# A two-layer decoder trunk on one core: rotary table and masks loaded behind the first four weight tiles, squares of the first norm ordered behind casts

## The chip, the cores and the metric

One Trainium2 chip, one NeuronCore of it. The metric is the device time of one execution in microseconds; the number told for a kernel is the median of its runs.

## The reference, cut to what matters

Two decoder layers on 256 tokens of width 2048, all in float32. Layer 0 is a norm, one wide input projection that feeds an RG-LRU group and an HGRN2 group of 8 heads, an output projection and an MLP; layer 1 has dilated attention in place of the two groups. The change touches only the first steps:

```python
h = x
hn = rms_norm(h, norm_mix[0])      # x * rsqrt(mean(x*x) + eps) * gain
proj = hn @ w_in                   # 2048 x 6144
x_lru, y_lru, q_h, f_h, v_h, g_h = jnp.split(proj, ...)
...
q = silu(q_raw); f = lower_bound + (1 - lower_bound) * sigmoid(f_raw)   # per HGRN2 head
```

The kernel multiplies by w_in before it knows the norm's factor: the gain is put on x beforehand, and the factor of each token (`rt`, and its transpose `rs`) is applied to the results.

## The kernel before, in words

Weights stream through the core in tiles of 128 x 2048 float32 (1024 KB). Each is loaded by SyncE's queue into a buffer `raw`, split by ScalarE into a rounded part `hi` (L104) and by VectorE into the rest `lo = raw - hi` (L105), in two halves of 1024 columns, and then used by TensorE in float32r matmuls (L187): activation-hi times hi, activation-lo times hi, activation-hi times lo. `raw`, `hi` and `lo` have three buffers each, so a new tile's cast to `hi` waits until TensorE is done with the tile three places before.

I number the weight tiles u0, u1, u2 and so on in the order of their use. u0 to u3 are the four tiles of the value group v0 (two PSUM accumulators, tokens on the partitions); u4, u5 and u6 are the q, f and g projections of HGRN2 head 0; u7 is the first RG-LRU projection; u8 to u10 are head 1. Every projection from u4 on takes one PSUM bank named `p` of a pool with three banks (`pmm`): v0 has the first and the second, u4 the third, u5 and u6 the first and second again, u7 the third again. A bank is free again when it has been read: v0's by the copy `vg` (L361), the banks of u4, u5 and u6 by the multiplication `hz = p * rs` (L425), whose factor `rs` (buffer `nr`, copied from PSUM at L379) comes from the first norm.

The opening (`fetch_first`) loads x and u0 to u3 in turns and in pieces: u0 in four pieces of 512 columns, u1 in two of 1024, u2 and u3 whole, each with its share of x ahead of it (L165 and L166). For each of the 16 blocks of x ScalarE writes the scaled rounded part into `bufa` (L248) and VectorE the rest (L249). `FirstNorm.add` squares each block of x on ScalarE (L280, tile `t`) and VectorE sums the squares in `q` (L283, L285); after the sixteenth, four pairs of small matmuls (L293) turn the sums into one number for each token, VectorE works out the reciprocal root in a chain of small operations (L295, L330 to L335), two transposes (L317) spread it, and ScalarE copies the result (L379). The transposes need the identity in `tab_` (L264), which also holds the rotary frequencies; the masks `msk` (L266) are read by the HGRN2 heads.

The order of instructions on each engine is fixed when the kernel is built, by a scheduler that goes by its own estimate of durations, by priorities (`high_priority`, `stream`, `urgent`) and by the dependencies it is given. `after(ins, names)` adds a dependency that costs no wait at run time and only fixes the order of two instructions on one engine. On the chip every engine works through its own list in order. SyncE's DMAs use eight semaphores in turn, so an issue also waits for the DMA eight places before.

Of the kernel before, what the change touches and what calls it, by code (L numbers as in the profile page):

```python
# [15 lines left out]
AF = mybir.ActivationFunctionType  # L16
# [25 lines left out]
def trunk_kernel(ctx, tc, x, xtok, cols, tab, masks, pos, fin, w_in, w_gate, w_out, w_qkv, w_o, w1, w2, out):  # L42
    nc = tc.nc
# [13 lines left out]
    V, A, T = nc.vector, nc.scalar, nc.tensor  # L57
# [8 lines left out]
    made = {}  # L66
# [10 lines left out]
    for step in ORDER.split():  # L77
        src, first, n = where[step[0]]
# [14 lines left out]
    class Weights:  # L93
# [7 lines left out]
        def split(self, at, n):  # L101
            h, l = self.part(at, n)
            w = self.raw[:, at:at + n]
            A.copy(h, w)  # L104
            i = V.tensor_tensor(l, w, h.bitcast(F32), OP.subtract)  # L105
            self.ins = getattr(i, "ins", i)

# [19 lines left out]
    def combine(u, src, i, what, i0):  # L127
        def load(name, j, home=wraw):
            held[name] = home.tile([P, 2048], F32, name="raw" if home is wraw else name)
            nc.sync.dma_start(held[name], src[j])  # L130

        def add(to, x, y):
            return V.tensor_tensor(held[to], held[x], held[y], OP.add)

        if what == "a":
            load("t1", i0 + 4, both)
            load("a", i)
            held["s"] = both.tile([P, 2048], F32, name="s")
            add("s", "a", "t1")
        elif what in ("n", "d"):  # L140
            load(what, i)
        def make(step=2048):
            made[u] = Weights(held[{"t1": "s", "t2": "s", "t3": "t1", "t4": "s"}.get(what, what)], step)

        ahead = units[u + 1][2:3] if u + 1 < len(units) else ()
        if ahead == ("t2",):
            load("c", i0 + 5)
            nc.gpsimd.dma_start(held["t1"], src[i0 + 5], accum_op=OP.add)
            add("s", "s", "c")
        make(2048 if src is w1 or what != "t2" else 0)  # L150
        if src is not w1 and what == "t2":
            waiting.append(made[u])
        if what == "c":
            nc.gpsimd.dma_start(held["s"], src[i0 + 1], accum_op=OP.add)

    def fetch_first():
        for u in range(4):
            at[0] += 1
            r = wraw.tile([P, 2048], F32, name="raw")
            src, i = units[u]  # L160
            n = (4, 2, 1, 1)[u]
            for m in range(n):
                ks = slice(4 * u + m * 4 // n, 4 * u + (m + 1) * 4 // n)
                ws = slice(m * 2048 // n, (m + 1) * 2048 // n)
                nc.sync.dma_start(xin[:, ks], x[:, ks])  # L165
                nc.sync.dma_start(r[:, ws], src[i][:, ws])  # L166
                if m == 0 and n > 1:
                    made[u] = Weights(r, 0)
                for k in range(ks.start, ks.stop):
                    split_to(bufa[:, k], xin[:, k], col("nmix0", k))  # L170
                if n > 1:
                    made[u].split(m * 2048 // n, 2048 // n)
                else:
                    made[u] = Weights(r, 1024)

    def unit(src, i):
        u = at[1]
        assert units[u][0] is src and units[u][1] in (None, i), (u, i)
        at[1] += 1
        if u + 2 >= at[0]:  # L180
            fetch()
        return made.pop(u)
# [24 lines left out]
    def after(ins, names):  # L207
        ins = getattr(ins, "ins", ins)
        for n in names:
            tc.add_manual_dep(ins, n, NOSYNC, reason="order on one engine")  # L210
        return ins.name
# [30 lines left out]
    def split_to(dst, src, gain=None):  # L242
        if gain is None:
            h, l = dst[..., :S], dst[..., S:]
            A.copy(h, src)  # L245
            V.tensor_tensor(l, src, h.bitcast(F32), OP.subtract)
        else:
            A.activation(dst[:, :S], src, AF.Copy, scale=gain)  # L248
            V.scalar_tensor_tensor(dst[:, S:], src, gain, dst[:, :S].bitcast(F32),  # L249
                                   op0=OP.mult, op1=OP.subtract)  # L250
# [9 lines left out]
    with tc.high_priority():  # L260
        nc.scalar.dma_start(c_, cols)
        fetch_first()
    tab_ = cst.tile([P, NTAB], F32, name="tab_")
    nc.sync.dma_start(tab_, tab)  # L264
    msk = cst.tile([P, NLEV, P], I8, name="msk")
    nc.sync.dma_start(msk, masks)  # L266
    ident = tab_[:, TC_ID:TC_ID + P]
    lnc = tab_[:, TC_LNC:TC_LNC + 384]
    epsc = cst.tile([P, 1], F32, name="epsc")
# [3 lines left out]
    class FirstNorm:  # L273
# [3 lines left out]
        def add(self, blk):  # L277
            self.n += 1
            q = wk.tile([P, S], F32, name="t1", bufs=2)
            A.activation(q, blk, AF.Square)  # L280
            if self.n == 1:
                self.ss.append(wk.tile([P, S], F32, name="q", bufs=1))
                V.tensor_copy(self.ss[0], q)  # L283
            elif self.n < KB:
                V.tensor_tensor(self.ss[0], self.ss[0], q, OP.add)  # L285
            else:
                self.ss.append(q)
# [293 lines left out]
    for step in ORDER.split():  # L581
        i = int(step[1])
# [324 lines left out]
    def values(i0):  # L907
# [16 lines left out]
        def final(n, j, bank):  # L924
            if (n, j) == (0, 1):
                with urgent():
                    A.activation(v[:, j, n], bank, AF.Copy, scale=rt[:, j:j + 1])
            elif (n, j) == (1, 0):
                add(n, j, bank, v[:, j, n], OP.subtract)
            else:  # L930
                add(n, j, bank, v[:, j, n], OP.add, scale=not n)
# [29 lines left out]
    with urgent():  # L961
        for j in range(2):
            m = tmp.tile([P, 1], F32, name="fm", bufs=2)
            r = tmp.tile([P, 1], F32, name="fr", bufs=2)
# [5 lines left out]
            i = V.scalar_tensor_tensor(m, ss[:, LAST:LAST + 1], 1.0 / D, m, op0=OP.mult, op1=OP.add)  # L970
            sums2.append(getattr(i, "ins", i).name)
            i = A.activation(t, m, AF.Sqrt)
# [6 lines left out]
        for j in range(2):  # L979
            for n, e in ((0, A), (LAST, V), (1, A if j else V), (3, V if j else A)):  # L980
# [4 lines left out]
                elif e is A:  # L985
                    i = A.activation(x_, x_, AF.Copy, scale=rr[j])
                    if n == 3:
                        after(i, roots[1:])
                else:
                    i = V.tensor_scalar(x_, x_, rr[j], None, op0=OP.mult)  # L990
# [118 lines left out]
```

## Time and profile before

| | |
|---|---|
| median of 3 runs | 2158.49 us (2158.27 to 2158.55) |
| the profiled execution's own time | 2158.39 us |
| its span | 2156.4 us, so 1.99 us lie around the span |
| TensorE matmul busy | 2140.6 us, 99% |
| VectorE busy | 1788.3 us, 83% |
| ScalarE busy | 1270.0 us, 59% |
| DMA | 485.64 MB, mean 225 GB/s |

In the profile PE is TensorE's matmuls, PEld its weight loads, DVE VectorE, ACT ScalarE, SP SyncE; a q behind an engine's name is its sequencer, which issues DMAs. All times count from the span's start. In a row of the timeline the first two numbers are the start and the duration in us, an x with a number tells how many instructions the row holds, and brackets give the idle time ahead of it and what ended that.

### The profile page before, as it was taken

The page shows a single profiled execution, that of the slowest core. Times are in us where ns is not written, and L with a number is a line of the kernel's source. Part 1 is how long each engine was busy: PE and PEld are TensorE (multiplying, and loading weights), DVE is VectorE, ACT ScalarE, POOL GpSimd, SP SyncE. Part 2 cuts the span into 40 slices and gives each one's busy share as a digit, 9 for nine tenths or more (in the row PEclk, how much of TensorE's full clock was granted, in tenths as well). Part 3 has the DMA queues.
Part 4 walks back from the last instruction along what each step waited for, and adds up shares of the span by engine and source line. Part 5 has one row for each costly group of instructions (what it writes and reads, how often), then busy time and mean ns, then how long its engine had stood idle before and what let it go on. Part 6 is the DMA issues. An engine that isn't in the chain of part 4 may idle for free.

```text
span 2156.4 us, 27736 instructions
## 1 busy us (share of the span) xinstructions
PE 2140.6 (99%) x11020; PEld 1831.1 (85%) x11020; DVE 1788.3 (83%) x2098; ACT 1270.0 (59%) x1415; POOL 61.9 (3%) x77
## 2 busy tenths in 40 slices
PE   9999999999999999999999999999999999999998
PEld 8999998888888888888888888888888888888886
DVE  7776787788888888889998897867988988888887
ACT  7444485566566566557665546456655755755764
POOL 0000000000000000000000000000000000000000
PEclk9999999999999999999999999999999999999999
DMA  8444445578878788887775546457778778788884
GB/s 320 157 157 158 156 157 214 177 234 273 247 241 258 255 247 239 277 246 236 247 258 196 175 160 232 157 183 227 236 241 278 243 241 264 254 247 244 265 262 153
DMA packets 68736, 485.64 MB, mean 225 GB/s; under 512 B 7664, under 2 KB 8432, under 8 KB 10624
## 3 DMA queue, kind: packets, MB, share of 16 engines
q1 hardware_dynamic: 58176, 410.89, 51.8%
q0 software_dynamic: 10144, 72.39, 18.1%
q8 instruction: 86, 1.41, 0.3%
q10 hardware_dynamic: 288, 0.61, 0.1%
q14 instruction: 42, 0.34, 0.0%
HBM read 481.76 MB, written 2.10 MB: 224 GB/s over the span
## 4 chain that ended last, share of the span: by engine, by line
PE 96%; DVE 2%; DMA 1%; ACT 1%; issue 0%; SPq 0%; DVEq 0%
PE p L187 66%; PE pd L187 12%; PE po L187 12%; PE pl L190 2%; PE pl L483 1%; DVE lo L105 1%; PE pt L187 1%; DMA raw<-in_w_in 1%; DMA raw<-in_w 0%; ACT hi L104 0%; PE pl L877 0%; PE po L898 0%; PE pd L890 0%; PE pd L467 0%; PE pl L876 0%
## 5 line engine op out<-in xcount | busy, mean ns | idle before, releaser
L104 ACT CAST hi<-raw 128x2048 fp32r<-128x2048 f32 (+2 forms) x468 | 683.8, 1484 | 552.1 <-PE p L187 345.4
L105 DVE TENSOR_TENSOR lo<-raw,hi 128x2048 fp32r<-128x2048 f32 (+2 forms) x468 | 816.7, 1760 | 221.9 <-ACT hi L104 206.3
L187 PE MATMUL p<-hi,bufb 128*128 128x512 f32 x1408 | 448.9, 391 | 0.5 <-ACT bufb L245 0.5
L187 PE MATMUL p<-hi,bufa 128*128 128x512 f32 x1136 | 366.4, 391 | 1.0 <-ACT hi L104 1.0
L187 PE MATMUL p<-bufa,hi 128*128 128x256 f32 (+1 forms) x1792 | 365.3, 317 | 0.1
L187 PEld LDWEIGHTS p<-hi,bufb 128*128 128x128 f32 x1408 | 264.3, 188 | 55.6 <-ACT bufb L245 0.7
L187 PEld LDWEIGHTS p<-bufa,hi 128*128 128x128 f32 x1792 | 294.2, 190 | 18.6 <-DVE hz L425 0.3
L187 PE MATMUL p<-lo,bufb 128*128 128x512 f32 x704 | 274.3, 390 | 0.7 <-DVE lo L105 0.7
L187 PE MATMUL p<-bufa,lo 128*128 128x256 f32 x1152 | 256.6, 287 | 0.0
L187 PEld LDWEIGHTS p<-hi,bufa 128*128 128x128 f32 x1136 | 213.5, 188 | 48.3 <-DVE y L727 2.4
L105 DVE TENSOR_TENSOR lo<-s,hi 128x2048 fp32r<-128x2048 f32 x102 | 233.1, 2286 | 17.9 <-ACT hi L104 15.8
L104 ACT CAST hi<-s 128x2048 fp32r<-128x2048 f32 x102 | 195.2, 1913 | 51.6 <-PE po L187 21.3
L187 PE MATMUL p<-lo,bufa 128*128 128x512 f32 x568 | 221.6, 390 | 1.8 <-DVE lo L105 1.8
L187 PEld LDWEIGHTS p<-bufa,lo 128*128 128x128 f32 x1152 | 189.7, 191 | 2.7
L187 PEld LDWEIGHTS p<-lo,bufb 128*128 128x128 f32 x704 | 132.2, 188 | 27.8 <-DVE lo L105 1.0
L187 PEld LDWEIGHTS p<-lo,bufa 128*128 128x128 f32 x568 | 106.8, 188 | 24.4 <-DVE lo L105 3.0
L187 PE MATMUL pd<-hi,bufa 128*128 128x512 f32 x288 | 95.3, 392 | 0.0
L187 PE MATMUL p<-hi,formx 128*128 128x512 f32 x288 | 94.9, 390 | 0.0
L105 DVE TENSOR_TENSOR lo<-t,hi 128x2048 fp32r<-128x2048 f32 x34 | 77.8, 2288 | 13.0 <-ACT hi L104 13.0
L187 PE MATMUL po<-hi,bufa 128*128 128x512 f32 x256 | 84.9, 393 | 0.0
L187 PE MATMUL p<-hi,formh 128*128 128x512 f32 x256 | 84.0, 389 | 0.0
L187 PE MATMUL pd<-hi,bufb 128*128 128x512 f32 x256 | 83.0, 389 | 0.0
(302 smaller groups left out, 2891.9 us busy)
## 6 DMA issues: line engine op xcount, KB each, us to landing
raw<-in_w SPq DMA_DIRECT2D x224, 1024.0 KB, 6.5
raw<-in_w_in SPq DMA_DIRECT2D x46, 1024.0 KB, 4.9
raw<-in_w_qkv SPq DMA_DIRECT2D x46, 1024.0 KB, 5.0
t<-in_w SPq DMA_DIRECT2D x32, 1024.0 KB, 6.4
t<-in_w POOLq DMA_DIRECT2D x32, 1024.0 KB, 8.8
s<-in_w POOLq DMA_DIRECT2D x32, 1024.0 KB, 9.2
raw<-in_w_out SPq DMA_DIRECT2D x16, 1024.0 KB, 4.9
raw<-in_w_o SPq DMA_DIRECT2D x16, 1024.0 KB, 4.9
```

The source lines that it names most:

```text
L104: A.copy(h, w)
L105: i = V.tensor_tensor(l, w, h.bitcast(F32), OP.subtract)
L187: chain[:] = [after(T.matmul(*args, **kw), chain)]
L190: chain[:] = [after(T.transpose(out_, in_, ident), chain)]
L483: T.matmul(pl[:, j], kq[:, js], halves(qp[:, js], c, True), start=True, stop=True)
```

## The change

Two things, both in the opening. First, the loads of `tab_` and `msk` get an order behind the last load of `fetch_first`, the weights of u3; before, they stood on SyncE's queue between the last piece of u0 and the first of u1. Second, each square of the first norm gets an order on ScalarE behind a cast of a weight tile: the squares 1 to 6 behind the last cast of u1, 7 to 12 behind that of u2, 13 to 16 behind that of u3. No operation is added or removed.

```diff
         def split(self, at, n):
             h, l = self.part(at, n)
             w = self.raw[:, at:at + n]
-            A.copy(h, w)
+            self.cast = after(A.copy(h, w), [])
...
+    loads, casts = [], []
+
     def fetch_first():
         for u in range(4):
...
                 nc.sync.dma_start(xin[:, ks], x[:, ks])
-                nc.sync.dma_start(r[:, ws], src[i][:, ws])
+                loads[:] = [after(nc.sync.dma_start(r[:, ws], src[i][:, ws]), [])]
...
                 else:
                     made[u] = Weights(r, 1024)
+            casts.append(made[u].cast)
...
-    nc.sync.dma_start(tab_, tab)
+    after(nc.sync.dma_start(tab_, tab), loads)
     msk = cst.tile([P, NLEV, P], I8, name="msk")
-    nc.sync.dma_start(msk, masks)
+    after(nc.sync.dma_start(msk, masks), loads)
...
             q = wk.tile([P, S], F32, name="t1", bufs=2)
-            A.activation(q, blk, AF.Square)
+            after(A.activation(q, blk, AF.Square), [casts[1 if self.n <= 6 else 2 if self.n <= 12 else 3]])
```

Because the scheduler lays out each engine's list anew with these orders, the lists of the built kernels differ beyond the lines that were touched, up to about the 290th row of TensorE's list; behind that they are the same. The prediction quotes from the new lists what it uses.

## The prediction

> **What bounds the kernel.** I read the page's busy shares and chain first.
>
> ```profile
> span 2156.4 us, 27736 instructions
> PE 2140.6 (99%) x11020; PEld 1831.1 (85%) x11020; DVE 1788.3 (83%) x2098; ACT 1270.0 (59%) x1415; POOL 61.9 (3%) x77
> PE 96%; DVE 2%; DMA 1%; ACT 1%; issue 0%; SPq 0%; DVEq 0%
> ```
>
> TensorE is busy for 99% of the span and carries 96% of the chain that ended last. So an edit in the opening counts by one thing: how much idle time of TensorE it takes away or adds. The second view is what TensorE waited for in the first 120 us, then the chain in order of time (start, length, what).
>
> ```profile
> PE p L187 <- DVE lo L105: 1.8, 3, 0.8
> PE po L259 <- DVE xp L535: 1.1, 1, 1.1
> PE p L187 <- ACT hi L104: 1.0, 2, 0.7
> ```
>
> ```profile
> 4.01 5.72 DMA raw<-in_w_in
> 9.73 0.02 issue
> 9.75 9.97 DMA raw<-in_w_in
> 19.72 0.02 issue
> 19.74 1.06 ACT hi L104
> 20.80 0.02 issue
> 20.82 1.24 DVE lo L105
> 22.06 0.04 issue
> 22.11 12.60 PE p L187 x61
> 34.70 0.79 PE pt L293 x8
> ...
> 42.54 0.22 PE pt L317 x2
> ...
> 52.47 0.45 PE pd L467 x4
> ```
>
> The chain is made of transfers until 19.72, when u2's weights have landed; then come u2's first cast, its remainder, and from 22.11 on TensorE without a break. Nothing that TensorE waits for lies between 22.11 and 120 us. So the opening has a gain to give only up to 22.11, and any new wait behind it is a loss in full.
>
> **Part one: table and masks behind u3.** The transfers are the limit there, by the windows (length, then busy time of PE, PEld, DVE, ACT, POOL, granted clock, DMA share, GB/s) and the table of DMA issues (the last number is the time from issue to landing).
>
> ```profile
> 6.20:10.00 3.80, 3.73 (x15) 2.55 (x14) 2.67 (x11) 2.57 (x6) 0.00 (x0) 1.00 1.00 324
> 10.00:15.00 5.00, 3.41 (x12) 2.10 (x12) 4.77 (x16) 4.27 (x11) 0.00 (x0) 1.00 1.01 351
> 15.00:20.00 5.00, 4.90 (x22) 4.06 (x23) 4.98 (x17) 3.77 (x9) 0.00 (x0) 1.00 1.02 423
> ```
>
> ```profile
> 4.49 0.43 SPq L264 DMA_DIRECT2D tab__181<-in_tab  x1
> 4.97 0.43 SPq L266 DMA_DIRECT2D msk<-in_masks  x1
> ...
> tab__181<-in_tab SPq DMA_DIRECT2D x1, 257.0 KB, 6.0
> msk<-in_masks SPq DMA_DIRECT2D x1, 80.0 KB, 5.7
> ```
>
> The DMA engines are full from 6.2 to 20, so what counts is the bytes ahead of u2's. u0's last piece landed at 9.73 (4.01 + 5.72); the table landed at 4.49 + 6.0 = 10.5 and the masks at 4.97 + 5.7 = 10.67. Together they held the transfers for 10.67 - 9.73 = 0.94 us. By bytes it would be 337 KB, 345 thousand bytes, at 423 to 324 GB/s: 0.82 to 1.06 us. Moved behind u3, they leave this time to u1, u2 and u3: u2 lands at about 18.8. Behind u2 come u3's x and weights, 1.57 MB, 3.7 us at 423 GB/s, so table and masks land at about 18.8 + 3.7 + 0.94 = 23.4. Their first readers are the two transposes (42.54 in the chain) and, for the masks, a head's work behind them: some 19 us of cover, cost nothing. If that cover were gone, the price would be the 0.94 us again.
>
> **Part two: squares behind the casts.** The squares leave ScalarE's and VectorE's lists ahead of u1.
>
> ```profile
> 12.14 0.71 ACT L280 ACTIVATE t<-xall 128x256 f32<-128x256 f32 x2
> 12.76 1.03 ACT L104 CAST hi<-raw 128x1024 fp32r<-128x1024 f32 x1
> 15.10 0.50 PE L187 MATMUL p<-lo,bufa 128*128 128x512 f32 x1 [0.75 <-DVE lo L105]
> ```
>
> Two squares, 0.36 us each, stood right ahead of u1's first cast, which had no idle time before it; it may have been held by up to that 0.7 us. But u1 is not the last wait: u2's is, and its cast followed the landing (19.72 to 19.74) without a square in between. For u2 the squares are worth nothing. Their sums do not hold it either: in the new list four of them stand ahead of u2's remainder, where ten stood before.
>
> TensorE's two waits on u2 are these:
>
> ```profile
> 20.84 0.19 PEld L187 LDWEIGHTS p<-hi,bufa 128*128 128x128 f32 x1 [0.66 <-ACT hi L104]
> 22.11 0.50 PE L187 MATMUL p<-lo,bufa 128*128 128x512 f32 x1 [0.76 <-DVE lo L105]
> ```
>
> So the opening gives 0.94 us if u2 follows its landing exactly, less 0 to 0.1 for VectorE, whose new list ahead of u2's remainder is just as long as the time until the cast ends: **I take 0.9**. The bounds are 0, if something other than the transfers set the landing, and 1.4, both waits gone whole (0.66 + 0.76).
>
> **What the squares are moved past.** The sixteen squares now spread from behind u1's cast to behind u7's, and the norm's chain with them. VectorE's new list, from the built kernel, reads:
>
> ```
> lo u7, lo u7, nm (L295), small chain ..., lo u8, rs, lo u8, rs, nr (chain ends), lo u9, lo u9, hz u4, hz u5, hz u6
> ```
>
> and ScalarE's: hi u7 twice, the last square, hi u8 twice, `vg` times factor twice, hi u9 twice, copy of `nr`. Before, the norm's chain ran among u6, and `hz` of u4 stood ahead of `lo` of u8:
>
> ```profile
> 43.06 0.36 ACT L379 COPY nr<-pt 128x256 f32<-128x256 f32 x1
> 44.51 0.42 DVE L425 TENSOR_TENSOR hz<-p,nr 128x256 f32<-128x256 f32 x1
> 45.54 1.99 ACT L104 CAST hi<-raw 128x1024 fp32r<-128x1024 f32 x2 [2.12 <-PE p L187]
> 46.62 2.36 DVE L105 TENSOR_TENSOR lo<-raw,hi 128x1024 fp32r<-128x1024 f32 x2 [0.54 <-ACT hi L104]
> ...
> 51.10 0.28 PE L187 MATMUL p<-bufa,lo 128*128 128x256 f32 x1
> 51.22 0.40 PE L187 MATMUL p<-bufa,hi 128*128 128x256 f32 x2
> ...
> 51.42 0.42 DVE L425 TENSOR_TENSOR hz<-p,nr 128x256 f32<-128x256 f32 x1 [0.50 <-PE p L187]
> ```
>
> These are `nr`, `hz` of u4, u8's two casts, u8's two remainders, u6's last matmul (51.10 to 51.38), u7's first two, and `hz` of u6, which starts as u6's last matmul is done. u7 needs the third PSUM bank, u4's. Before, that bank was free at 44.51 + 0.42 = 44.9, 6.3 us ahead of u7's start at 51.22. Now its reader stands behind `lo` of u9; that waits for `hi` of u9, in the buffer that u6 used, and so for u6's last matmul. u7's first matmul thus waits for a chain that can start only when u6 has ended, and TensorE, in order, has nothing else in front of it. The chain's length is in the rows of u8, which went the same way: cast released by TensorE at 45.54, remainders from 46.62 to 48.98, 3.44 us, then 0.42 for `hz`: 3.86, less 0.05 of overlap, plus some 0.1 for the two signals between engines. It starts when u6's last matmul ends, 0.28 us after that was issued; u7's first would have been issued 0.12 us after it (51.10, 51.22), so 0.16 us are added. The norm's two transposes (0.22 us, in the chain at 42.54, among u5) now stand between u6 and u7; they run inside the wait and are gone elsewhere, which takes 0.22 off. The wait is 3.86 - 0.05 + 0.1 + 0.16 - 0.22 = 3.85 us: **I take 3.8**. Bounds: not less than ScalarE's own list, two casts 2.0, `nr` 0.36, `hz` 0.42 and signals 0.1, 2.9; not more than 4.2, with 0.3 for further signals. Queued behind `hz` on VectorE is head 0's work; its first matmuls stand some 2.7 us behind u7's start in TensorE's list, and need `hz`, a sigmoid and one multiplication, about 1.4 us: not late. Behind that the lists are the old ones, so the shift stays to the end.
>
> The token-ordered x (`xall<-in_xtok`) waits for the last square and goes three weight tiles later on SyncE's queue. Its first reader is the residual of the output projection, far behind; u10 queues behind it, three tiles ahead of TensorE's use of it. Cost nothing; without that cover it would be its own transfer, 2 MB at 423 GB/s, 5 us.
>
> **Sum.** Against the profiled execution: 2158.39 - 0.9 + 3.8 = 2161.3 us, and the runs' median is 0.1 above that execution, which I leave out as within their spread. That is 0.13% slower; 0.2%, or 4.3 us, is about what a measurement of this kernel can tell from no change, so it counts as within.
>
> **Rivals.** *The wait does not come, only the gain:* 2158.39 - 0.9 = 2157.5. It asks that `hz` of u4 run ahead of u6's end; the 6.3 us of room before speak for it, the fixed list against it. Chance 0.06. *The opening gains nothing* (another transfer holds u2): 2162.2. The full DMA windows speak against it; chance 0.04. *Slower, by the clock:* TensorE's clock falls when it idles long enough.
>
> ```profile
> 2146.60:2150.30 3.70, 0.00 (x0) 0.00 (x0) 3.35 (x10) 2.62 (x6) 0.00 (x0) 1.00 0.17 69
> 2150.40:2156.40 6.00, 0.00 (x0) 0.00 (x0) 0.46 (x2) 0.65 (x2) 0.00 (x0) 0.50 0.76 301
> ```
>
> ```profile
> 1.05 5.49 PE L259 MATMUL po<-ones 128*128 128x128 f32 x24 [1.05 <-DVE xp L535]
> ```
>
> At the end TensorE stood still from 2146.6, and by 2150.4, 3.8 us later, the granted clock was 0.50; the opening's waits of up to 0.8 us did not lower it (1.00 in the windows above). A stop of 3.8 us at u7 is at this very length. The cold price: the warm-up passes took 5.49 / 24 = 0.229 us, passes of the same size later 0.45 / 4 = 0.112 (L467, in the chain), so half speed, for at most the 5.5 us of the warm-up: 2.8 us lost, and none at the least. That gives 2161.3 + 2.8 = 2164.1, slower by 0.26%. It decides from about 3.7 us of stop on; since matmul tails and the transposes shorten the true stop to about 3.6, I give it 0.12. The Trainium skill, "TensorE: Matmul & The Clock Gate", section "Part 1: The HAM clock gate", says that the gate halves the clock after one wholly idle window of about 3.4 us, of windows that run freely, and restores it after a busy one; an estimate by that page is 1.7 us of loss, 2163.0, and only if a whole window falls into the stop. By that rule the trace's 3.8 us fits, and nothing here shows a stop in between.
>
> **How the numbers follow.** The forecast has the rest, 0.78. Its own range is 2158.39 - 1.4 + 2.9 = 2159.9 to 2158.39 + 4.2 = 2162.6; I stretch the upper end to 2163.2 to take in the milder half of the clock's case. Faster by over 0.2% (below 2154.2) follows from no case: 0.01. Slower (above 2162.8): the clock's 0.12, and 0.01 for a longer chain. Within: 0.86.
>
> **What would show it.** Right: in the profile after, TensorE starts u2's remainders near 21.2 and has one new wait of 3.7 to 3.9 us near 50 to 54 us, at L190, put down to `hz`; everything behind 60 us is later by 2.9. Wrong: no such wait, or one put down to something else; u2 still near 22; or a granted clock below 1 behind the wait.

## The result, and the profile after

| | before | changed |
|---|---|---|
| median of 11 runs each | 2158.49 us (2157.86 to 2159.28) | 2162.9 us (2161.78 to 2163.95) |
| profiled execution | 2158.39 us, span 2156.4 | 2163.38 us, span 2161.4 |
| ratio of the times | | 1.0021, 95% interval 1.0013 to 1.0028 |

The changed kernel is slower by 4.4 us, 0.21%. The first view is what TensorE waited for in the first 120 us (total, times, longest), in the changed kernel; L190 is the L187 of before, L428 its L425.

```profile
PE p L190 <- DVE hz L428: 3.5, 1, 3.5
PE p L190 <- DVE lo L105: 2.0, 4, 0.8
PE po L262 <- DVE xp L538: 1.1, 1, 1.1
```

One wait is new, 3.5 us, and it is put down to `hz`. The timeline around it:

```profile
49.38 0.38 PE L320 MATMUL pt<-tab__181,nr 128*128 128x128 f32 x2
49.47 1.99 ACT L104 CAST hi<-raw 128x1024 fp32r<-128x1024 f32 x2 [0.61 <-PE p L190]
50.54 2.36 DVE L105 TENSOR_TENSOR lo<-raw,hi 128x1024 fp32r<-128x1024 f32 x2 [3.06 <-ACT hi L104]
51.37 0.36 ACT L382 COPY nr<-pt 128x256 f32<-128x256 f32 x1
...
52.82 1.07 DVE L428 TENSOR_TENSOR hz<-p,nr 128x256 f32<-128x256 f32 x3
...
53.29 0.80 PE L190 MATMUL p<-bufa,hi 128*128 128x256 f32 x2 [3.53 <-DVE hz L428]
```

The casts of u9 start as u6's last matmul ends, the two remainders follow, then the three `hz`, and with the first of them u7 starts. The last row holds a second thing: the two matmuls of u7 take 0.80 us, where before two took 0.40. The windows name it (length, busy times, and third from the end the granted clock):

```profile
48.80:49.70 0.90, 0.90 (x9) 0.72 (x7) 0.00 (x0) 0.29 (x2) 0.00 (x0) 1.00 0.80 291
49.80:52.10 2.30, 0.00 (x0) 0.00 (x0) 1.56 (x2) 2.28 (x4) 0.00 (x0) 1.00 0.73 278
52.30:53.20 0.90, 0.00 (x0) 0.00 (x0) 0.90 (x3) 0.73 (x1) 0.00 (x0) 0.50 0.13 55
53.30:55.60 2.30, 2.30 (x11) 2.30 (x12) 2.23 (x8) 1.33 (x4) 0.00 (x0) 0.50 0.78 203
55.70:59.00 3.30, 3.30 (x17) 3.30 (x17) 0.66 (x4) 0.00 (x0) 0.00 (x0) 0.50 0.41 174
59.10:62.00 2.90, 2.90 (x26) 2.90 (x26) 0.76 (x2) 0.00 (x0) 0.00 (x0) 1.00 0.00 0
```

TensorE's clock fell to half at about 52.2, when TensorE had stood still for only 2.4 us, and stayed there for 6.8 us, of which TensorE worked 5.7. The chain of waits shows the price:

```profile
49.47 1.05 ACT hi L104
50.54 2.36 DVE lo L105 x2
52.90 0.34 DVE hz L428
53.29 5.28 PE p L190 x23
58.57 0.72 PE pd L470 x4
```

23 matmuls in 5.28 us would be 23 x 0.12 = 2.76 us at full clock, and the four passes of `pd` 0.45 us: together 2.8 us lost. The opening, on the other side, gained: u2's remainders are used from 20.43 on, where it was 22.11.

```profile
20.43 0.50 PE L190 MATMUL p<-lo,bufa 128*128 128x512 f32 x1 [0.75 <-DVE lo L105]
```

### The profile page after: what moved, and what is told of

Read it like the earlier page. It is cut to its first block, busy times and chain, and to the rows that moved or that the text cites. A ratio compares the mean times of both kernels' runs of the same rounds, so it can differ in the third digit from the quotient of the medians.

```text
span 2161.4 us, 27741 instructions
## 1 busy us (share of the span) xinstructions
PE 2142.5 (99%) x11020; PEld 1832.5 (85%) x11020; DVE 1788.2 (83%) x2098; ACT 1270.0 (59%) x1415; POOL 61.9 (3%) x77
## 3 DMA queue, kind: packets, MB, share of 16 engines
q1 hardware_dynamic: 58176, 410.89, 52.2%
## 4 chain that ended last, share of the span: by engine, by line
PE 95%; DVE 2%; ACT 1%; DMA 1%; issue 1%; SPq 0%; DVEq 0%
PE p L190 66%; PE pd L190 12%; PE po L190 12%; PE pl L193 2%; PE pl L486 1%; DVE lo L105 1%; PE pt L190 1%; DMA raw<-in_w 0%; ACT hi L104 0%; PE pl L880 0%; DMA raw<-in_w_in 0%; PE po L901 0%; PE pd L893 0%; PE pd L470 0%; PE pl L879 0%
## 5 line engine op out<-in xcount | busy, mean ns | idle before, releaser
L190 PE MATMUL p<-hi,bufb 128*128 128x512 f32 x1408 | 448.9, 391 | 0.5 <-ACT bufb L248 0.5
L190 PE MATMUL p<-bufa,hi 128*128 128x256 f32 (+1 forms) x1792 | 367.6, 318 | 3.6 <-DVE hz L428 3.5
L190 PE MATMUL p<-hi,bufa 128*128 128x512 f32 x1136 | 365.8, 391 | 0.0
L190 PEld LDWEIGHTS p<-bufa,hi 128*128 128x128 f32 x1792 | 296.0, 192 | 22.4 <-DVE hz L428 4.0
L190 PEld LDWEIGHTS p<-hi,bufb 128*128 128x128 f32 x1408 | 264.3, 188 | 55.6 <-ACT bufb L248 0.7
L190 PE MATMUL p<-lo,bufb 128*128 128x512 f32 x704 | 274.3, 390 | 0.9 <-DVE lo L105 0.9
L190 PE MATMUL p<-bufa,lo 128*128 128x256 f32 x1152 | 257.5, 288 | 0.0
L190 PEld LDWEIGHTS p<-hi,bufa 128*128 128x128 f32 x1136 | 213.3, 188 | 46.9 <-DVE y L730 2.4
L190 PE MATMUL p<-lo,bufa 128*128 128x512 f32 x568 | 221.7, 390 | 2.1 <-DVE lo L105 2.0
L190 PEld LDWEIGHTS p<-bufa,lo 128*128 128x128 f32 x1152 | 190.7, 192 | 2.7
L190 PEld LDWEIGHTS p<-lo,bufb 128*128 128x128 f32 x704 | 132.2, 188 | 28.0 <-DVE lo L105 1.2
L190 PEld LDWEIGHTS p<-lo,bufa 128*128 128x128 f32 x568 | 106.7, 188 | 25.3 <-DVE lo L105 3.8
L190 PE MATMUL pd<-hi,bufa 128*128 128x512 f32 x288 | 95.3, 392 | 0.0
L190 PE MATMUL p<-hi,formx 128*128 128x512 f32 x288 | 94.9, 390 | 0.0
L190 PE MATMUL po<-hi,bufa 128*128 128x512 f32 x256 | 84.9, 393 | 0.0
L190 PE MATMUL p<-hi,formh 128*128 128x512 f32 x256 | 84.0, 389 | 0.0
L190 PE MATMUL pd<-hi,bufb 128*128 128x512 f32 x256 | 83.0, 389 | 0.0
```

What stands on the lines that cost most here:

```text
L190: chain[:] = [after(T.matmul(*args, **kw), chain)]
```

## Experiments

The kernel before ran beside each of these: 2158.33 us (2157.71 to 2159.16, 32 runs) beside the first four, 2158.37 us (2157.60 to 2159.44, 27 runs) beside the others. The comparisons have about 0.09% of uncertainty; where a conclusion rests on less, the profile carries it.

| run | median, us | range, us | stop ahead of u7 | clock behind it |
|---|---|---|---|---|
| tables alone | 2157.0 | 2156.66 to 2157.77 | none | 1.00 |
| squares alone | 2163.9 | 2163.03 to 2165.21 | 3.5 | 0.50 for 3.4 us |
| changed, 16 filling matmuls | 2160.46 | 2160.00 to 2160.87 | filled | 1.00 |
| changed, norm's chain released | 2157.51 | 2156.91 to 2158.39 | none | 1.00 |
| changed, 8 filling | 2160.77 | 2160.48 to 2162.00 | 1.7 | 1.00 |
| changed, 4 filling | 2161.05 | 2159.76 to 2162.92 | 2.6 | 0.50 for 3.4 us |
| changed, u9 alone held back | 2158.92 | 2158.34 to 2159.64 | 0.9 | 1.00 |

Stop and clock are those of the one profiled execution.

**Each half of the change by itself.** Tables alone takes the order of the squares out of the changed kernel:

```diff
-            after(A.activation(q, blk, AF.Square), [casts[1 if self.n <= 6 else 2 if self.n <= 12 else 3]])
+            A.activation(q, blk, AF.Square)
```

> Only the table and the masks are moved behind u3; the squares are left where the kernel before has them. My reading (the opening's gain belongs to the transfers, the loss to the squares): u2's first remainder is used near 20.4 to 21.2 us in place of 22.11, TensorE has no wait of over 1 us behind 23 us, the granted clock stays at 1.00, and the time is 0.9 to 1.7 us below the kernel before, 2156.8 to 2157.6. Rival (the squares ahead of u1's cast held the opening): u2 stays near 22 us and the time near 2158.5.

Squares alone takes the order of the loads out:

```diff
-    after(nc.sync.dma_start(tab_, tab), loads)
+    nc.sync.dma_start(tab_, tab)
-    after(nc.sync.dma_start(msk, masks), loads)
+    nc.sync.dma_start(msk, masks)
```

> Only the order of the squares; table and masks stand where the kernel before has them. My reading: u2's first remainder is used near 22.1 us, TensorE stops for about 3.7 us ahead of u7 (near 51 to 55 us), the clock falls to 0.50 for 3.4 to 6.8 us behind that, and the time is 2158.5 + 3.7 + 2.6 = 2164.8, 2163.9 to 2165.3. Rival (the squares give part of the opening's gain): u2 is used 0.5 us or more earlier than 22.1, and the time is 2164.2 or less.

Tables alone came out 1.3 us below the kernel before (ratio 0.9994, interval 0.9985 to 1.0003, which does not exclude no change; but its slowest run lies only 0.06 us above the fastest of before). What TensorE waited for, and u2's way, in tables alone:

```profile
PE p L190 <- DVE lo L105: 1.4, 4, 0.8
PE po L262 <- DVE xp L538: 1.1, 1, 1.1
```

```profile
17.17 2.00 ACT L104 CAST hi<-raw 128x1024 fp32r<-128x1024 f32 x2
...
18.46 1.23 DVE L105 TENSOR_TENSOR lo<-raw,hi 128x1024 fp32r<-128x1024 f32 x1
...
19.74 0.50 PE L190 MATMUL p<-lo,bufa 128*128 128x512 f32 x1 [0.17 <-DVE lo L105]
```

No stop, and u2's remainders are used at 19.74, earlier than in the changed kernel and than the 20.4 to 21.2 expected. Squares alone has the stop, and a clock that falls:

```profile
PE p L190 <- DVE hz L428: 3.5, 1, 3.5
...
```

```profile
50.60:53.90 3.30, 0.00 (x0) 0.00 (x0) 2.62 (x4) 3.15 (x4) 0.00 (x0) 1.00 0.57 211
54.10:57.30 3.20, 3.20 (x15) 3.20 (x16) 2.94 (x12) 1.27 (x4) 0.00 (x0) 0.50 0.88 284
57.50:60.00 2.50, 2.50 (x24) 2.50 (x22) 0.76 (x2) 0.00 (x0) 0.00 (x0) 1.00 0.07 30
```

So the whole loss belongs to the order of the squares, and nearly all of the gain to the order of the loads, with the lists that the scheduler lays out for it. The time, 2163.9, is at the lower end of what was expected; in the one execution profiled the clock stayed down for 3.4 us and not 6.8, and 23 matmuls of u7 took 4.49 us and not 5.28, so about 1.7 us were lost there. By the letter, the rival that the squares give part of the opening's gain met both its marks: u2's remainders are used at 21.16, 0.9 before the 22.1 of the first profile, and the time is below 2164.2. My own mark, u2 near 22.1, missed. But the second profile of the kernel before, below, has u2 at 21.35 with the same order of loads, and against it the squares give 0.2 us, by one execution each.

**The stop filled, but not shortened.** Behind u6's matmuls, in an unused part of its bank:

```diff
         (acc or cross)(p, w, jobs)
+        if at[1] == 7:
+            for _ in range(16):
+                mm(p[:, S:S + P], ones, ones, start=True, stop=True)
         return p
```

> The changed kernel with 16 float32 matmuls of 128 columns more, about 0.225 us each, which stand in TensorE's list between u6 and u7, write an unused part of u6's bank, and so fill the stop without shortening it. My reading (the clock fell because TensorE stood still): u7 starts when it did, near 53.3 us, TensorE's idle time ahead of it is under 0.4 us, the clock stays at 1.00, and the time is that of the changed kernel less the slow stretch, 2162.9 - 2.6 = 2160.3, 2159.8 to 2160.9. Rival (the clock's fall has another cause, or the loss behind the stop is not the clock's): 2162.5 or more.

2160.46, as expected. u7 starts as long after u2's remainders as it did (20.34 to 53.20, in the changed kernel 20.43 to 53.29), but TensorE is at work until then and its clock does not fall:

```profile
50.40 2.84 PE L190 MATMUL p<-ones 128*128 128x128 f32 x24
53.20 0.50 PE L190 MATMUL p<-bufa,hi 128*128 128x256 f32 x2
```

```profile
49.40:53.20 3.80, 3.80 (x35) 3.65 (x33) 2.75 (x4) 3.54 (x5) 0.00 (x0) 1.00 0.52 211
53.40:60.00 6.60, 6.60 (x57) 6.60 (x57) 3.86 (x15) 1.52 (x5) 0.00 (x0) 1.00 0.48 161
```

Work that computes nothing makes the kernel 2.4 us faster (2162.9 to 2160.46). That is the clock's part of the loss. The filled kernel's slowest run, 2160.87, is faster than the fastest of the changed kernel, 2161.78. So the clock probably fell in all 11 runs of the changed kernel; a profile shows it for one.

**How long a stop the clock bears.** The same with 8 and with 4.

```diff
-            for _ in range(16):
+            for _ in range(8):      # and, in another kernel, range(4)
```

> As the kernel with 16 filling matmuls, but with 8, so that TensorE stands still for about 1.9 us ahead of u7 in place of 0.2. Theory one (the clock falls only after a window of 3.4 us without any work): the clock stays at 1.00 in every run, and all times are near 2160.5. Theory two (a window with little work is enough, as the changed kernel's own clock record has it, where the window that ended at 52.2 us had work in its first 0.98 us): a stop of 1.9 us can take at most 56% of a window; if the clock falls, it costs 1.7 to 3.4 us, and times lie at 2162 and more in some or all runs.

> The same with 4 filling matmuls, a stop of about 2.8 us, up to 82% of a window. Theory one: the clock stays at 1.00 in every run, all times near 2160.5. Theory two: the clock falls in a good part of the runs, where the stop lies mostly in one window; the times then fall into two groups, near 2160.5 and near 2162 to 2163.5.

A window of the kernel with 8, behind its stop:

```profile
53.30:60.00 6.70, 6.70 (x56) 6.70 (x57) 3.96 (x15) 1.62 (x5) 0.00 (x0) 1.00 0.44 159
```

The windows of the kernel with 4:

```profile
50.50:53.00 2.50, 0.00 (x0) 0.00 (x0) 2.50 (x4) 2.29 (x3) 0.00 (x0) 1.00 0.40 157
53.50:56.80 3.30, 3.30 (x18) 3.30 (x17) 2.58 (x11) 0.91 (x3) 0.00 (x0) 0.50 0.90 315
57.00:60.00 3.00, 3.00 (x27) 3.00 (x27) 0.76 (x2) 0.00 (x0) 0.00 (x0) 1.00 0.00 0
```

A stop of 2.6 us was enough here, so theory one falls. The clock fell at 53.5, when TensorE had been back at work for 0.4 us. The 11 times spread from 2159.76 to 2162.92, over 3 us where the kernel with 16 spreads over 0.9, as if the clock fell in some runs and not in others; they do not part into two clear groups. With 8, a stop of 1.7 us, the profiled execution kept its clock, and eight of 11 runs lie between 2160.48 and 2160.95. Of the other three, two owe their length to time around the span: 2161.29 and 2162.00 have spans of 2158.6 and 2158.9 us, as in the kernel with 16 (2158.1 to 2158.9), with 2.7 and 3.1 us around them, where the other kernels have 1.8 to 2.1. Only the third, 2161.80, has a longer span, 2159.6; whether the clock fell in it stays open.

What ran last ahead of the stop in the kernel with 4, and in the changed kernel, were the norm's two transposes (0.38 us). No run tells whether they count as work for the clock; without them the two stops are 0.2 to 0.3 us longer.

**The norm's chain released.** `squares` holds the names of the squares in order.

```diff
-            self.cast = after(A.copy(h, w), [])
+            self.cast = after(A.copy(h, w), squares[9:10] if count[0] == 5 else squares[-1:])
```

> The changed kernel, with one order more on ScalarE: the casts of u4 behind the tenth square, and those of all later tiles behind the sixteenth, so that the norm's chain is not spread over u4 to u9. My reading: hz of u4 is done well ahead of u6's end, TensorE does not stop ahead of u7, the clock stays at 1.00, and only the opening's gain is left: 0.9 to 1.7 us below the kernel before, 2156.8 to 2157.6. Rival (part of the loss belongs to the late token-ordered x, or to the table landing late): over 2158.5 though the stop is gone.

2157.51, without the stop, within what was expected:

```profile
PE p L192 <- DVE lo L107: 2.0, 4, 0.8
PE po L264 <- DVE xp L540: 1.1, 1, 1.1
PE p L192 <- ACT hi L106: 0.3, 1, 0.3
```

The table still lands behind u3, and nothing waits for it: its late landing costs nothing here.

**Only u9 held back.** `spread` holds the copy of `nr`; the squares stay late.

```diff
-            self.cast = after(A.copy(h, w), [])
+            self.cast = after(A.copy(h, w), spread if count[0] == 10 else [])
...
-    A.copy(rs, over_tokens(rt))
+    spread.append(after(A.copy(rs, over_tokens(rt)), []))
```

> The changed kernel with one order more: the casts of u9 behind the copy of nr on ScalarE. The squares stay as late as the change puts them; VectorE's list then has hz of u4 ahead of the remainders of u9. My reading (the stop comes from hz standing behind a tile that waits for u6, not from the norm being late): the stop shrinks from 3.7 to about 1.1 us or less, the clock stays at 1.00, and the time is 2157.0 + 1.1 = 2158.1, 2157.0 to 2158.6. Rival (the late squares themselves hold u7): the stop stays over 2.5 us and the time over 2160.

```profile
PE p L192 <- DVE lo L107: 1.9, 4, 0.8
PE po L264 <- DVE xp L540: 1.1, 1, 1.1
PE p L192 <- DVE hz L430: 0.9, 1, 0.9
```

The stop shrank from 3.5 to 0.9 us with the squares as late as in the changed kernel. So it was the place of `hz` behind a tile that waits for u6, and not the late norm, that made the stop; the lateness is worth the 0.9 that is left. The time, 2158.92, is 0.3 above the range expected. That range started from tables alone, where u2's remainders are used at 19.74; here, with the squares late, they are used at 21.01.

**The kernel before, once more.**

> The kernel before, for a second look at its opening. If the landing of u2's weights at 19.72 us is what this order of loads gives, it lands at 19.5 to 19.9 again; if it differs from execution to execution, it lands nearer to 18.0, where the kernel with the same order of loads and later squares had it, and the table and masks are worth the difference to 17.2, about 0.85 us, and not 1.7.

```profile
18.02 2.00 ACT L104 CAST hi<-raw 128x1024 fp32r<-128x1024 f32 x2
19.14 0.42 DVE L285 TENSOR_TENSOR q<-q,t 128x256 f32<-128x256 f32 x1
19.66 0.43 DVE L285 TENSOR_TENSOR q<-q,t 128x256 f32<-128x256 f32 x1
...
20.08 1.22 DVE L105 TENSOR_TENSOR lo<-raw,hi 128x1024 fp32r<-128x1024 f32 x1
...
21.35 0.50 PE L187 MATMUL p<-lo,bufa 128*128 128x512 f32 x1 [0.84 <-DVE lo L105]
```

u2's weights, issued at 9.48, landed 8.5 us later, at 18.0, this time, 1.7 us earlier than in the first profile, and its first use of the remainder moved by only 0.8, to 21.35, since VectorE was busy with sums of squares. The execution took 2157.94, 0.45 less than the first profiled one.

## Why the prediction was right and where it was wrong

The measured 2162.9 lies inside the stated range of 2159.9 to 2163.2, but above 2162.6, where the range that follows from the terms ended. It lies inside only by the stretch that was added for the clock, and its nearness to the forecast is in part luck: the forecast left out 2.4 us of clock, and 0.8 us that the opening gained beyond what was taken made up for a part of it. Of the marks named beforehand, the place of the new wait and `hz` as its cause came; u2's remainders came at 20.43 and not near 21.2, the wait as counted is 3.5 and not 3.7 to 3.9, the span grew by 5.0 and not 2.9, and a granted clock below 1, named as a sign of being wrong, came too.

**The opening, 0.9 us: the size was right by luck, its reason half.** Against the second profile of before the changed kernel gains 21.35 - 20.43 = 0.92 us at u2; against the first, from which the 0.9 was taken, it gains 1.7. Table and masks are worth in landing about what was worked out: 18.0 with them ahead in two executions (19.7 in the third), 17.2 without (in six kernels 17.0 to 17.5, in one 17.8). But the step that the squares and their sums are worth nothing for u2, and do not hold it, failed. Without the squares' order the gain is larger: u2 at 19.74, 21.35 - 19.74 = 1.6 us. About half of that is the landing; the rest is VectorE's list, which was laid out anew there too and has one sum fewer between u2's cast and its remainder than in the kernel before. With the squares' order it is 0.7 less; in the six kernels with late squares and the table behind u3, u2's remainders are used between 20.20 and 21.01. The changed kernel's rows show why:

```profile
17.02 0.42 DVE L288 TENSOR_TENSOR q<-q,t 128x256 f32<-128x256 f32 x1
...
17.53 0.42 ACT L283 ACTIVATE t<-xall 128x256 f32<-128x256 f32 x1 [0.43 <-DVE q L288]
...
17.85 1.99 ACT L104 CAST hi<-raw 128x1024 fp32r<-128x1024 f32 x2
```

u2's weights, issued at 8.56, had landed 8.7 us later, by 17.3. Its cast waited until 17.85 behind a square, and that square for VectorE's sum, which frees one of two `t` buffers. The order that was to clear the way for casts put a square, and with it a wait for VectorE, right ahead of one. The first profile of before, on which the prediction rested, hid this: its late landing gave VectorE time to clear its list.

**The stop, 3.8 us: right**, in place, cause and length. From u2's remainders to u7's start it is 53.29 - 20.43 = 32.86 us, before 51.22 - 22.11 = 29.11: 3.75 longer, of which the profile counts 3.5 as a wait. The kernel with u9 alone held back shows the cause.

**Table, masks, token-ordered x at no cost: right.** The released kernel keeps the table late and runs at 2157.51. The token-ordered x was only seen not to be waited for, not tried by itself.

**The clock: the step that failed.** It was a rival with a chance of 0.12, because the stop was taken to have to last about 3.7 us. The runs show that it needs less: it fell 2.4 us into the stop, and in the kernel with 4 filling matmuls a stop of 2.6 us was enough. The price worked out for that rival, 2.8 us, is what the profiled execution lost; the medians say 2.4, and the execution of squares alone lost 1.7. The match is luck in part: the price was taken from the length of the warm-up, 5.5 us, and what was paid hung on whether the clock stayed down for 3.4 or 6.8 us. With the 22.11 - 20.43 = 1.7 us by which these two profiles differ in the opening, the terms close: 2158.39 - 1.7 + 3.8 + 2.8 = 2163.3, against 2163.38. The forecast of 2161.3 is thus the changed kernel without its clock, 2160.46, and 0.8 more, as much as it had missed of the opening's gain. The chance of being slower by over 0.2% was worked out with that low chance for the clock, and came out far too small for a case that lies right at that bound.

The rule of the Trainium skill that stood beside it ("TensorE: Matmul & The Clock Gate", section "Part 1: The HAM clock gate") is borne out in the length of its windows and not in its condition. The clock was down for 6.8 us once and 3.4 us twice, one or two windows of the page's 3.4. In the traces' clock records the stretch of full clock ahead of the fall is 47.79 us long in all three kernels in which it fell, 14 times 3.41. But if windows are that long and the clock falls at the end of one, the one that ended at 52.2 began at 48.8, and TensorE worked in it until 49.7. It was not wholly idle, as the prediction had read the page.

## What to carry to other kernels

An order that moves work of one step behind a step with a buffer cycle can close a circle: look, on each engine's new list, for an operation that frees a bank and now stands behind an operation that waits for the last user of another buffer. Price a stop of TensorE of 2.6 us or more, the shortest that lowered the clock here, with the clock added: 1.7 to 2.8 us in the executions here, on top of the stop. Take the opening from more than one profile: here one landing moved by 1.7 us between two executions of one kernel. Of what was run, the loads' order alone has the lowest median: 2157.0 us against 2158.33 before, hardly clear of no change, and 2162.9 for the change as a whole.

## What the runs showed of the hardware that was not expected

- TensorE's clock fell 0.4 us behind a stop of 2.6 us, and 2.4 us into a longer one; a stop of 1.7 us left it up in the one execution profiled.
- Back at work, TensorE did not get its full clock at the next turn: in the changed kernel the clock stayed at 0.50 from 52.2 to 59.0 though TensorE worked from 53.29 on. Where the clock fell at 54.0, just as work began again, it was up after 3.4 us.
- The same loads in the same order landed u2's weights at 19.7 in one execution and at 18.0 in another.
